# A decoder layer's expert inputs: each weight tile against 256-column activations in three products, gelu straight from PSUM

## The chip, the cores and the metric

The kernel runs on one core of one Trainium2 chip. What counts is the device time of one execution in microseconds (us). Five engines work side by side: TensorE (PE, with its weight loads listed apart as PEld), VectorE (DVE), ScalarE (ACT), GpSimd (POOL) and SyncE (SP), which issues most DMA transfers.

## What is computed

One layer of a decoder with 256 tokens and 2048 channels. It has an attention and a convolution branch, and then a layer of experts. The change touches the expert layer only. Cut to that, the reference is:

```
h2 = rms_norm(x, norm2_g) * (1 + scale2) + shift2
q = h2 @ w_q;  s = q . sub_keys           # scores, 8 heads x 2 halves x 128 keys
gate, expert = top 16 of 16 x 16 pairs, softmax over the scores
a = einsum('td,ted->te', h2, u_emb[expert])
coef = gelu(a) * gate
out = x + gate2 * einsum('te,ted->td', coef, v_emb[expert])
```

There are 128 x 128 = 16384 experts, and `u_emb` and `v_emb` have a row of 2048 for each.

## The kernel before

The experts are not gathered. The kernel computes the gelu of every expert's input for every token, multiplies it by a gate that is zero where the expert was not chosen, and multiplies the result by all of `v_emb`. So the expert layer is dense: 128 tiles of 128 experts against h2 (the **expert-input stage**, `u_tile`, called 128 times), and then all coefficients against `v_emb` (the **output stage**, `products`).

All large weights come through one class, `Stream`. SP loads chunks of 128 x 1024 floats (`raw`, four buffers). For each 512 columns of a chunk ACT casts the numbers to a shorter float (`hi`, L153, five buffers) and DVE subtracts to get the rest (`lo`, L159, four buffers), so that a product of two floats is made of three products of short ones: hi x hi, hi x lo and lo x hi. `prefetch` issues these casts three pieces ahead. A **piece** is the use of one such 512-column pair: four blocks of the contraction with 128 weight columns each. A weight tile of 128 experts is four pieces (16 blocks of 128 channels).

`proj` (L200 to L202) is the usual form: for each block one 256-column product of `hi` with the high activations, one of `hi` with the low ones, one of `lo` with the high ones. Each has its own weight load. The query heads (`head_q`), among others, use it. `proj2` (L213, L217) is used by `u_tile` alone. There h2 lies in one tile with the high and the low activations of a block side by side, so `hi` meets both in one 512-column product, and the sums are in the two halves of a PSUM bank; `lo` then meets the high ones in 256 columns.

After each piece, `step` moves the jobs on that stand in a list; a job is a generator that issues a few instructions and yields. So the order of instructions on all engines is fixed by the program, by how many pieces have gone by. The jobs in the expert-input stage are

- the evacuation of each tile (`f` in `u_tile`): ACT (the first 48 tiles) or DVE copies the second half of the bank into `ut`, DVE adds the first half, and ACT takes the gelu into the coefficient tile `C`. Where gates are already there (`n` tokens of 256), it is taken in two parts, and DVE multiplies the first part into `C`;
- in the first 48 tiles, `top_steps` on DVE: the top 16 of each head;
- then `g_steps`, 64 times: for four tokens, DVE makes one-hot tiles, ACT scales them, PE multiplies them (L1247, eight products of 128 columns in f16, the **one-hot products**) and DVE and ACT bring the result into `C`.

The scores of a head are one small group of f32 products (L1078, eight passes, the **head product**); that of the last head is issued within the first tile of the expert-input stage. Three pairs of transposes (L1140) come at the end of `top_steps`.

Of the kernel before, what the change touches and what calls it, by code (L numbers as in the profile page):

```python
# [9 lines left out]
F32 = mybir.dt.float32  # L10
F32R = mybir.dt.float32r
F16 = mybir.dt.float16
U32 = mybir.dt.uint32
AF = mybir.ActivationFunctionType
# [5 lines left out]
T = 256  # L20
D = 2048
KT = 16
# [50 lines left out]
def build(nc, tc, d):  # L73
    ctx = ExitStack()
    ve, sc, pe, sp = nc.vector, nc.scalar, nc.tensor, nc.sync
# [53 lines left out]
    class Stream:  # L129
# [63 lines left out]
        def proj(self, bank, nk, xhi, xlo, evac):  # L193

            ps = bank()
            for k0 in range(0, nk, 4):
                def mm(hi, lo):
                    for j in range(4):
                        k, o = k0 + j, j * 128
                        pe.matmul(ps, hi[:, o:o + 128], xhi[:, k], start=(k == 0), stop=False)  # L200
                        pe.matmul(ps, hi[:, o:o + 128], xlo[:, k], start=False, stop=False)  # L201
                        pe.matmul(ps, lo[:, o:o + 128], xhi[:, k], start=False, stop=(k == nk - 1))  # L202
                self.piece(mm)
            return self.add(evac(ps))

        def proj2(self, bank, nk, x, evac):

            ps = bank()
            for k0 in range(0, nk, 4):
                def mm(hi, lo):  # L210
                    for j in range(4):
                        k, o = k0 + j, j * 128
                        pe.matmul(ps.rearrange("p a t -> p (a t)"), hi[:, o:o + 128],  # L213
                                  x[:, k].rearrange("p a t -> p (a t)"), start=(k == 0), stop=False)
                    for j in range(4):
                        k, o = k0 + j, j * 128
                        pe.matmul(ps[:, 1], lo[:, o:o + 128], x[:, k, 0], start=False, stop=(k == nk - 1))  # L217
                self.piece(mm)
            return self.add(evac(ps))

# [33 lines left out]
    S = Stream(plan)  # L254
# [37 lines left out]
    def bank_st(shape):  # L292
        return ps_st.tile(shape, F32, name="ps_st", tag="st", bufs=1)

    ps = bank_st([128, T])
# [175 lines left out]
    def gen_bank(shape, tag="t", bufs=2):  # L471
        return ps_mix.tile(shape, F32, name="ps_" + tag, tag=tag, bufs=bufs)
# [470 lines left out]
    UC = T + 2  # L943
    gg = P("gg", side="right")
    h2p = P("h2p", side="right")
    h2 = h2p.tile([128, KT, 2, T], F32R, name="h2")
    h2hi, h2lo = h2[:, :, 0], h2[:, :, 1]
    np_ = P("np", side="right")
    rs2 = np_.tile([128, T], F32, name="rs2")
    hgate = np_.tile([128, 16], F32, name="hgate")  # L950
# [92 lines left out]
    HALF = 48  # L1043
# [143 lines left out]
    tokens, ready = [0], [0]  # L1187

    def u_tile(i1):
        def f(ps):  # L1190
            n = tokens[0]
            cs = C[0][:, i1] if i1 < HALF else C[1][:, i1 - HALF]
            t = gg.tile([128, T], F32, name="ut", tag="ut", bufs=1)
            if i1 < HALF:
                sc.copy(t, ps[:, 1])
            else:
                ve.tensor_copy(t, ps[:, 1])
            yield
            ve.tensor_add(t, t, ps[:, 0])
            yield  # L1200
            n = tokens[0]
            if n < T:
                sc.activation(cs[:, n:], t[:, n:], AF.Gelu_apprx_tanh)
            if n > 0:
                sc.activation(t[:, 0:n], t[:, 0:n], AF.Gelu_apprx_tanh)
            ready[0] = i1 + 1
            yield
            if n > 0:
                ve.tensor_mul(cs[:, 0:n], cs[:, 0:n], t[:, 0:n])
            yield  # L1210
        return S.proj2(lambda: gen_bank([128, 2, T], "acc"), KT, h2, f)

    def g_steps():

# [57 lines left out]
    for i1 in range(HALF):  # L1272
        u_tile(i1)
# [16 lines left out]
    for i1 in range(HALF, NK):  # L1290
        end = u_tile(i1)
# [164 lines left out]
```

## Time and profile before

| | us |
|---|---|
| median of 3 runs | 2449.55 |
| lowest, highest | 2449.41, 2452.64 |
| the profiled execution | 2450.68 |
| its span, first to last instruction | 2448.9 |
| PE busy | 2424.4 (99%) |
| DVE busy | 1935.9 (79%) |
| ACT busy | 1433.1 (59%) |

The profile shows one execution. The length of a matmul in it is longer than its share of the time, since matmuls overlap: a 256-column one is shown with some 0.28 us and the next one starts 0.11 us after it. What a stretch of matmuls costs is therefore read from the starts in the timeline, or from a window's length and the count of matmuls in it.

### The profile page before, as it was taken

What the parts mean: (1) busy time and instruction counts of PE and PEld (TensorE: products, weight loads), DVE (VectorE), ACT (ScalarE), POOL (GpSimd) and SP (SyncE); (2) the same over time, 40 slices, a digit from 0 to 9 for tenths busy, and PEclk for the clock granted to TensorE, in tenths of its full rate; (3) what the DMA queues carried; (4) which work ended last, traced back from release to release, by engine and by line L of the source; (5) the groups of instructions that cost most, each with busy time, mean ns of one, the idle gap of its engine ahead of it and who ended that gap; (6) DMA issues with size and microseconds to landing.
All of it is one profiled execution on the core that took longest, in us unless ns stands there. A gap on an engine that the chain in (4) does not pass through costs nothing.

```text
span 2448.9 us, 44266 instructions
## 1 busy us (share of the span) xinstructions
PE 2424.4 (99%) x15324; PEld 2151.9 (88%) x15324; DVE 1935.9 (79%) x4120; ACT 1433.1 (59%) x3214; POOL 144.0 (6%) x269
## 2 busy tenths in 40 slices
PE   8999999999999999999999999999999999999999
PEld 6899999888999999988888888888888888888887
DVE  7979887889788877999988888888655566666666
ACT  2145456767555566555568888888555555555554
POOL 0000000211222200000000000000000001000100
PEclk9999999999999999999999999999999999999999
DMA  9966556755899975555555555555555567777766
GB/s 384 405 217 197 178 190 196 241 176 186 301 319 322 319 263 173 184 190 190 191 184 177 176 177 176 174 178 174 191 191 193 190 211 244 240 245 240 243 205 195
DMA packets 155668, 540.50 MB, mean 221 GB/s; under 512 B 18866, under 2 KB 19122, under 8 KB 155314
## 3 DMA queue, kind: packets, MB, share of 16 engines
q1 hardware_dynamic: 134178, 467.40, 56.2%
q0 software_dynamic: 21264, 70.27, 9.3%
q8 instruction: 120, 1.97, 0.3%
q14 instruction: 106, 0.86, 0.1%
HBM read 533.41 MB, written 4.19 MB: 220 GB/s over the span
## 4 chain that ended last, share of the span: by engine, by line
PE 92%; DMA 4%; DVE 3%; issue 1%; SPq 0%; ACT 0%; DVEq 0%
PE ps_acc L213 20%; PE ps_acc L217 10%; PE acc L200 9%; PE acc L202 9%; PE acc L201 9%; DMA wa<-in_w_ada_dram 4%; PE ps_o L1335 2%; PE ps_s L1335 2%; PE ps_t L1335 2%; PE ps_o L1334 2%; PE ps_s L1334 2%; PE ps_t L1334 2%; PE ps_acc L1335 2%; PE ps_acc L1334 2%; PE ps_t L1336 2%; PE ps_o L1336 2%
## 5 line engine op out<-in xcount | busy, mean ns | idle before, releaser
L153 ACT CAST hi<-raw 128x512 fp32r<-128x512 f32 x1548 | 954.2, 620 | 802.2 <-PE acc L201 228.7
L159 DVE TENSOR_TENSOR lo<-raw,hi 128x512 fp32r<-128x512 f32 x1548 | 1064.4, 689 | 387.3 <-ACT hi L153 80.2
L213 PE MATMUL ps_acc<-h,hi 128*128 128x512 f32 x2048 | 564.6, 397 | 0.0
L213 PEld LDWEIGHTS ps_acc<-h,hi 128*128 128x128 f32 x2048 | 347.0, 188 | 44.2
L217 PEld LDWEIGHTS ps_acc<-h,lo 128*128 128x128 f32 x2048 | 311.5, 188 | 46.1
L200 PE MATMUL acc<-hhi,hi 128*128 128x256 f32 x1200 | 345.9, 288 | 0.0
L202 PE MATMUL acc<-hhi,lo 128*128 128x256 f32 x1200 | 333.0, 278 | 0.2 <-DVE lo L159 0.2
L201 PE MATMUL acc<-hlo,hi 128*128 128x256 f32 x1200 | 333.0, 277 | 0.0
L217 PE MATMUL ps_acc<-h,lo 128*128 128x256 f32 x2048 | 318.1, 277 | 0.0
L200 PEld LDWEIGHTS acc<-hhi,hi 128*128 128x128 f32 x1200 | 225.9, 188 | 6.3 <-issue 5.3
L201 PEld LDWEIGHTS acc<-hlo,hi 128*128 128x128 f32 x1200 | 226.1, 188 | 3.2 <-issue 3.1
L202 PEld LDWEIGHTS acc<-hhi,lo 128*128 128x128 f32 x1200 | 225.4, 188 | 0.4 <-DVE lo L159 0.4
L391 POOL DMA_DIRECT2D adaw<-in_w_ada_dram x192 | 104.7, 546 | 760.5 <-DVE rr L739 276.9
L405 DVE SCALAR_TENSOR_TENSOR ada<-adaw,sc_c,ada 128x512 f32<-128x512 f32 x180 | 134.5, 747 | 13.6 <-DMA adaw<-in_w_ada_dram 13.3
L1311 POOL DMA_DIRECT2D g2w<-in_w_ada_dram x64 | 34.3, 537 | 1404.4 <-DVE Alo L123 1098.5
L491 DVE SCALAR_TENSOR_TENSOR cacc<-glu,dwh,cacc 128x256 f32<-128x256 f32 x240 | 107.2, 491 | 0.0
L1226 ACT ACTIVATE Ahi<-ohA,high 128x128 f16<-128x128 f16 x256 | 100.7, 393 | 10.9 <-PE ps_o L1247 10.5
L359 PE MATMUL zb<-hr,w 128*128 128x256 f32 x448 | 103.9, 391 | 3.1 <-ACT hr L339 3.1
L359 PEld LDWEIGHTS zb<-hr,w 128*128 128x128 f32 x448 | 86.1, 195 | 15.0 <-ACT hr L339 3.4
L1226 ACT ACTIVATE Alo<-ohA,low 128x128 f16<-128x128 f16 x256 | 99.1, 387 | 0.0
L323 DVE SCALAR_TENSOR_TENSOR acc<-wa,sc_c,acc 128x256 f32<-128x256 f32 x224 | 91.3, 480 | 2.1 <-DMA wa<-in_w_ada_dram 2.1
L200 PE MATMUL acc<-mhi,hi 128*128 128x256 f32 x256 | 71.5, 279 | 0.0
(371 smaller groups left out, 4529.9 us busy)
## 6 DMA issues: line engine op xcount, KB each, us to landing
raw<-in_u_dram SPq DMA_DIRECT2D x256, 512.0 KB, 3.6
raw<-in_v_dram SPq DMA_DIRECT2D x256, 512.0 KB, 4.6
raw<-in_w_in_dram SPq DMA_DIRECT2D x150, 512.0 KB, 4.3
adaw<-in_w_ada_dram POOLq DMA_DIRECT2D x192, 256.0 KB, 5.1
wa<-in_w_ada_dram SPq DMA_DIRECT2D x64, 512.0 KB, 9.9
raw<-in_nsa_out_dram SPq DMA_DIRECT2D x32, 512.0 KB, 6.2
raw<-in_w_out_dram SPq DMA_DIRECT2D x32, 512.0 KB, 5.4
raw<-in_peer_wq_dram SPq DMA_DIRECT2D x32, 512.0 KB, 4.1
```

What stands on the lines that cost most here:

```text
L153: sc.copy(hi, self.source(n))
L159: ve.tensor_sub(lo, self.source(n), hi.bitcast(F32))
L200: pe.matmul(ps, hi[:, o:o + 128], xhi[:, k], start=(k == 0), stop=False)
L201: pe.matmul(ps, hi[:, o:o + 128], xlo[:, k], start=False, stop=False)
L202: pe.matmul(ps, lo[:, o:o + 128], xhi[:, k], start=False, stop=(k == nk - 1))
L213: pe.matmul(ps.rearrange("p a t -> p (a t)"), hi[:, o:o + 128], x[:, k].rearrange("p a t -> p (a t)"), start=(k == 0), stop=False)
L217: pe.matmul(ps[:, 1], lo[:, o:o + 128], x[:, k, 0], start=False, stop=(k == nk - 1))
L359: pe.matmul(zb[n // 2][:, n % 2], ws[k][n // 7][:, n % 7], hr[k], start=(k == 0 and n % 2 == 0), stop=(k == KT - 1), skip_group_check=True)
L405: ve.scalar_tensor_tensor(acc, raw, sc_c[:, k:k + 1], acc, op0=OP.mult, op1=OP.add)
L1226: sc.activation(part[:, j], A[:, j], AF.Copy, scale=g[:, t0 + j:t0 + j + 1])
L1334: pe.matmul(ps, chi, hi, start=(i1 == 0), stop=False)
L1335: pe.matmul(ps, chi, lo, start=False, stop=False)
```

## The change

`proj2` goes, and `u_tile` calls `proj` on two separate tiles, `h2hi` and `h2lo`. A tile's PSUM is 256 columns wide, and gelu reads it directly; the copy and the addition go.

```diff
-        def proj2(self, bank, nk, x, evac):
-
-            ps = bank()
-            for k0 in range(0, nk, 4):
-                def mm(hi, lo):
-                    for j in range(4):
-                        k, o = k0 + j, j * 128
-                        pe.matmul(ps.rearrange("p a t -> p (a t)"), hi[:, o:o + 128],
-                                  x[:, k].rearrange("p a t -> p (a t)"), start=(k == 0), stop=False)
-                    for j in range(4):
-                        k, o = k0 + j, j * 128
-                        pe.matmul(ps[:, 1], lo[:, o:o + 128], x[:, k, 0], start=False, stop=(k == nk - 1))
                 self.piece(mm)
             return self.add(evac(ps))
...
-    h2 = h2p.tile([128, KT, 2, T], F32R, name="h2")
-    h2hi, h2lo = h2[:, :, 0], h2[:, :, 1]
+    h2hi = h2p.tile([128, KT, T], F32R, name="h2hi")
+    h2lo = h2p.tile([128, KT, T], F32R, name="h2lo")
...
             cs = C[0][:, i1] if i1 < HALF else C[1][:, i1 - HALF]
-            t = gg.tile([128, T], F32, name="ut", tag="ut", bufs=1)
-            if i1 < HALF:
-                sc.copy(t, ps[:, 1])
-            else:
-                ve.tensor_copy(t, ps[:, 1])
-            yield
-            ve.tensor_add(t, t, ps[:, 0])
-            yield
-            n = tokens[0]
             if n < T:
-                sc.activation(cs[:, n:], t[:, n:], AF.Gelu_apprx_tanh)
+                sc.activation(cs[:, n:], ps[:, n:], AF.Gelu_apprx_tanh)
             if n > 0:
-                sc.activation(t[:, 0:n], t[:, 0:n], AF.Gelu_apprx_tanh)
+                t = gg.tile([128, T], F32, name="ut", tag="ut", bufs=1)
+                sc.activation(t[:, 0:n], ps[:, 0:n], AF.Gelu_apprx_tanh)
             ready[0] = i1 + 1
...
-        return S.proj2(lambda: gen_bank([128, 2, T], "acc"), KT, h2, f)
+        return S.proj(lambda: gen_bank([128, T], "acc"), KT, h2hi, h2lo, f)
```

How the order of instructions changes is seen best on PE. First at the beginning of the expert-input stage, from its first product to the head product (L1078 before, L1063 after) and a little beyond; `acc` and `ps_acc` are the PSUM tiles, `h_10305` is the interleaved h2. Before:

```order
L202 MATMUL acc<-h_10305,lo 128x256
L213 MATMUL ps_acc<-h_10305,hi 128x512 x4
L217 MATMUL ps_acc<-h_10305,lo 128x256 x4
L213 MATMUL ps_acc<-h_10305,hi 128x512 x4
L217 MATMUL ps_acc<-h_10305,lo 128x256 x4
L1078 MATMUL ps_s<-skT,pq 128x128 x4
L213 MATMUL ps_acc<-h_10305,hi 128x512 x4
L217 MATMUL ps_acc<-h_10305,lo 128x256 x4
```

And now, from the last two blocks ahead of the head product on:

```order
L200 MATMUL ps_acc<-h2hi,hi 128x256
L201 MATMUL ps_acc<-h2lo,hi 128x256
L202 MATMUL ps_acc<-h2hi,lo 128x256
L200 MATMUL ps_acc<-h2hi,hi 128x256
L201 MATMUL ps_acc<-h2lo,hi 128x256
L202 MATMUL ps_acc<-h2hi,lo 128x256
L1063 MATMUL ps_s<-skT,pq 128x128 x4
L200 MATMUL ps_acc<-h2hi,hi 128x256
L201 MATMUL ps_acc<-h2lo,hi 128x256
L202 MATMUL ps_acc<-h2hi,lo 128x256
```

The head product stays where it was, after two pieces; each piece has twelve products of one width in place of four wide and four narrow ones.

Second on PE, in the later part of the stage, the end of the one-hot products (L1247 before, L1224 after) and what follows them. Before:

```order
L1247 LDWEIGHTS ohB
L1247 MATMUL ps_o<-Ahi,ohB 128x128
L1247 LDWEIGHTS ohB
L1247 MATMUL ps_o<-Alo,ohB 128x128
L213 MATMUL ps_acc<-h_10305,hi 128x512 x4
L217 MATMUL ps_acc<-h_10305,lo 128x256 x4
```

And now:

```order
L1224 LDWEIGHTS ohB
L1224 MATMUL ps_o<-Ahi,ohB 128x128
L1224 LDWEIGHTS ohB
L1224 MATMUL ps_o<-Alo,ohB 128x128
L200 MATMUL ps_acc<-h2hi,hi 128x256
L201 MATMUL ps_acc<-h2lo,hi 128x256
L202 MATMUL ps_acc<-h2hi,lo 128x256
```

What follows an interruption is now a run of 256-column products.

On DVE, a tile in the later part of the stage (`C_13041` and `C_16353` are the two halves of the coefficients). Before:

```order
L1197 COPY ut<-ps_acc 128x256
L159 TENSOR_TENSOR lo<-raw,hi 128x512
L1220 TENSOR_TENSOR ohB<-cst,I2T 128x512
L1199 TENSOR_TENSOR ut<-ut,ps_acc 128x256
L159 TENSOR_TENSOR lo<-raw,hi 128x512
L1235 TENSOR_TENSOR C_13041<-C_13041,ps_o 128x48x4
L1235 TENSOR_TENSOR C_16353<-C_16353,ps_o 128x51x4
L159 TENSOR_TENSOR lo<-raw,hi 128x512
L1209 TENSOR_TENSOR C_16353<-C_16353,ut 128x176
```

And now:

```order
L159 TENSOR_TENSOR lo<-raw,hi 128x512
L1197 TENSOR_TENSOR ohB<-cst,I2T 128x512
L1186 TENSOR_TENSOR C_16981<-C_16981,ut 128x172
L159 TENSOR_TENSOR lo<-raw,hi 128x512
L1212 TENSOR_TENSOR C_13042<-C_13042,ps_o 128x48x4
L1212 TENSOR_TENSOR C_16981<-C_16981,ps_o 128x52x4
```

The copy and the addition are gone, and the product with the gates stands two pieces earlier. SP's transfers keep their order.

## Rows read from the trace of the kernel before

**Rows 1.** The page: busy us, share of the span, instructions; granted clock in tenths.

```profile
PE 2424.4 (99%) x15324; PEld 2151.9 (88%) x15324; DVE 1935.9 (79%) x4120; ACT 1433.1 (59%) x3214; POOL 144.0 (6%) x269
...
PEclk9999999999999999999999999999999999999999
```

**Rows 2.** Windows: stretch, length, busy us (count) of PE, PEld, DVE, ACT, POOL; clock.

```profile
1002.00:1252.00 250.00, 250.00 (x1443) 218.33 (x1442) 236.45 (x711) 142.12 (x272) 0.00 (x0) 1.00 0.58 190
1272.00:1740.00 468.00, 468.00 (x3013) 410.19 (x3013) 384.85 (x801) 374.88 (x1035) 0.00 (x0) 1.00 0.54 177
1741.00:2009.00 268.00, 268.00 (x1173) 219.94 (x1172) 152.82 (x248) 136.51 (x245) 2.12 (x4) 1.00 0.60 195
2010.00:2400.00 390.00, 390.00 (x1722) 322.88 (x1722) 266.47 (x426) 201.11 (x361) 32.19 (x60) 1.00 0.72 235
```

**Rows 3.** The tile `ut`: count; ns least/median/most; first and last start; forms.

```profile
L1199 DVE TENSOR_TENSOR ut<-ut,ps_acc x128: 399/414/419, 1004.4 to 1742.4; 128x256 f32<-128x256 f32 x128
L1203 ACT ACTIVATE C<-ut x123: 193/370/421, 1006.0 to 1715.2; 128x256 f32<-128x256 f32 x49, 128x240 f32<-128x240 f32 x2, 128x216 f32<-128x216 f32 x2, 128x192 f32<-128x192 f32 x2
L1197 DVE COPY ut<-ps_acc x80: 415/419/425, 1269.4 to 1741.2; 128x256 f32<-128x256 f32 x80
...
L1195 ACT COPY ut<-ps_acc x48: 354/367/368, 1001.8 to 1263.3; 128x256 f32<-128x256 f32 x48
```

**Rows 4.** Timeline of PE, steady pieces: start us, length us, engine, line, count.

```profile
1102.81 1.09 PE L213 MATMUL ps_acc<-h,hi 128*128 128x512 f32 x4
1103.74 0.62 PE L217 MATMUL ps_acc<-h,lo 128*128 128x256 f32 x4
...
1111.13 1.09 PE L213 MATMUL ps_acc<-h,hi 128*128 128x512 f32 x4
```

**Rows 5.** Timeline of PE behind the last head product.

```profile
997.90 1.05 PE L1078 MATMUL ps_s<-skT,pq 128*128 128x128 f32 x8
...
999.72 0.63 PE L217 MATMUL ps_acc<-h,lo 128*128 128x256 f32 x4
1000.19 1.10 PE L213 MATMUL ps_acc<-h,hi 128*128 128x512 f32 x4
```

**Rows 6.** Timeline of PE at one set of one-hot products.

```profile
1406.11 0.23 PE L1247 MATMUL ps_o<-Ahi,ohB 128*128 128x128 f16 x1
...
1406.54 1.18 PE L213 MATMUL ps_acc<-h,hi 128*128 128x512 f32 x4
1407.56 0.62 PE L217 MATMUL ps_acc<-h,lo 128*128 128x256 f32 x4
1408.02 1.09 PE L213 MATMUL ps_acc<-h,hi 128*128 128x512 f32 x4
```

**Rows 7.** Timeline of PE, query heads: first and last of three stretches.

```profile
963.65 0.28 PE L200 MATMUL acc<-h,hi 128*128 128x256 f32 x1
...
973.74 0.28 PE L202 MATMUL acc<-h,lo 128*128 128x256 f32 x1
...
975.10 0.28 PE L200 MATMUL acc<-h,hi 128*128 128x256 f32 x1
...
985.81 0.28 PE L201 MATMUL acc<-h,hi 128*128 128x256 f32 x1
...
987.64 0.28 PE L200 MATMUL acc<-h,hi 128*128 128x256 f32 x1
...
995.01 0.28 PE L202 MATMUL acc<-h,lo 128*128 128x256 f32 x1
```

**Rows 8.** Timeline of PE behind four transposes: first and last of a stretch.

```profile
633.00 0.28 PE L201 MATMUL acc<-hlo,hi 128*128 128x256 f32 x1
...
665.87 0.28 PE L200 MATMUL acc<-ohi,hi 128*128 128x256 f32 x1
```

**Rows 9.** Timeline: one `lo`, and the first products of its piece.

```profile
1199.84 0.68 DVE L159 TENSOR_TENSOR lo<-raw,hi 128x512 fp32r<-128x512 f32 x1
...
1202.65 1.09 PE L213 MATMUL ps_acc<-h,hi 128*128 128x512 f32 x4
```

More of the change, by code (lines that the diff above doesn't have):

```diff
@@ L202, in mm @@
                         pe.matmul(ps, lo[:, o:o + 128], xhi[:, k], start=False, stop=(k == nk - 1))
-                self.piece(mm)
-            return self.add(evac(ps))
-        def proj2(self, bank, nk, x, evac):
-            ps = bank()
-            for k0 in range(0, nk, 4):
-                def mm(hi, lo):
-                    for j in range(4):
-                        k, o = k0 + j, j * 128
-                        pe.matmul(ps.rearrange("p a t -> p (a t)"), hi[:, o:o + 128],
-                                  x[:, k].rearrange("p a t -> p (a t)"), start=(k == 0), stop=False)
-                    for j in range(4):
-                        k, o = k0 + j, j * 128
-                        pe.matmul(ps[:, 1], lo[:, o:o + 128], x[:, k, 0], start=False, stop=(k == nk - 1))
                 self.piece(mm)
```

## The prediction

> **What bounds the kernel now.** I read the page first: PE is busy for 99% of the span and the granted clock is full in every slice [rows 1]. Since busy time of pipelined matmuls says little, I went on to the stage that the change touches. The expert-input stage runs from about 995 to 1740 us. In the windows inside it PE shows no idle time, while DVE and ACT both have some [rows 2]; the waits of PE in this stretch are an empty list. So the stage lasts as long as its matmuls take from start to start, and I need their pace, which the timeline gives.
>
> I call the work on one quarter of a weight tile (four k blocks, one `hi` and one `lo` tile) a piece. 128 expert tiles of 4 pieces make 512 pieces. A piece before is four 512-column products (L213) and four 256-column products (L217). Six pieces in a row begin at 1102.81 and end at 1111.13, so a piece lasts 1.387 us: 0.93 for the four wide products, 0.457 for the four narrow ones [rows 4]. The window agrees: 250 us hold 1443 matmuls, 8 a piece, 1.386 us each [rows 2]. In the second part, from about 1271 us, the one-hot products (eight f16 matmuls, 64 times) cut in: 0.43 us, and the wide group behind them takes 1.02 instead of 0.93, so 0.52 us a time [rows 6]. Check: 3013 matmuls, 8 a piece and 8 an interruption, are 376.6 of both, and at 1.387 and 0.52 us the 468 us contain 63 interruptions [rows 2].
>
> **What the new piece costs.** It is twelve 256-column products, each with its own weight load, the form that `proj` already runs in the query heads just ahead, on the same h2. There the trace shows two paces (columns of the rows: start, length, engine, line). From 963.65 to 973.74 there are 90 such matmuls, 89 gaps of 113.4 ns; from 975.10 to 985.81 there are 92, 91 gaps of 117.7 ns [rows 7]. Both have a granted clock of 2.4 GHz, the same form and the same tiles. I call them the short and the long pace. Twelve of the short make 1.360 us a piece, twelve of the long 1.413 us: 0.027 us less or 0.026 us more than before. Over 512 pieces that is -13.8 or +13.3 us, so the whole question is which pace the stage falls into.
>
> What chooses? In these rows the pace changes only where other matmuls cut in (the head's eight short f32 passes, L1078) and then holds. Between these two stretches stands one head product; behind the next one it is short again, 66 matmuls with 65 gaps of 113.4 ns from 987.64 to 995.01 [rows 7]: the sides alternate. Behind transposes in an earlier stage the short pace held for 291 matmuls, 290 gaps of 113.3 ns, from 633.00 to 665.87 [rows 8].
>
> First part of the stage, up to the first one-hot product at about 1271 us. The last head product is issued two pieces into the stage, in the old order and the new one, and the stretch ahead of it is short; by alternation it is followed by the long pace. The old rows agree: behind that product (997.90) the four narrow matmuls take 0.47 us, which is 4 x 117.7, against 0.45 to 0.46 in the steady state [rows 4, 5]. Before, the wide products then bring the pattern back; in the new stream nothing follows but more 256-column products, until three pairs of transposes shortly before 1271 us. So I take the long pace for 190 pieces: 190 x 0.026 = +4.9 us. If it broke at once it would be 190 x -0.027 = -5.1 us.
>
> Second part, 320 pieces. Behind the one-hot products the wide group is 0.09 us late and the narrow group takes 0.46 us, not 0.47 [rows 6]: the pattern comes back on the short side. I read that as the short pace for the new stream: 320 x -0.027 = -8.6 us. No 256-column product of this type stands behind f16 ones in the trace, so both ends stay open: +8.3 us if it is long each time. I keep the 0.09 us for the restart and add 0.01 us (two gaps at the long pace) 64 times, +0.6 us; the ends are nothing and +2.3 us (eight long gaps).
>
> **Edits at nothing.** 48 ACT copies of 0.367 us, 80 DVE copies of 0.419 and 128 DVE additions of 0.414 go [rows 3]: 17.6, 33.5 and 53.0 us of engine time, all beside a PE that does not pause [rows 2], so 0. The cover is PE itself: were the feeders late, this would be the reserve. The two gelus read PSUM where they read `ut`; a copy from PSUM on ACT costs 0.367 us, a gelu from SBUF 0.370 [rows 3], so a moved read costs nothing either. The gelu now waits on ACT for the last matmul of its tile. Queued behind it are the casts to `hi`. But the cast just ahead of it waits for the same piece to give its buffer back, so nothing is added.
>
> What gets tighter is the weights. `lo` was first read 0.93 us into a piece and is now read by the third matmul, 0.23 us in; `hi` is given back by the eleventh of twelve matmuls, at 1.25 us, not at 0.93. In the piece with the least lead, in the first part where DVE is busy 236 of 250 us, `lo` ends at 1200.52 and the piece begins at 1202.65 [rows 2, 9]. That leaves 2.13 + 0.23 = 2.36 us where the new stream needs it, and DVE has 53 us less to do, so I charge 0. If it failed, the price would be a stop of some tenths of a us in up to 190 pieces. Weights are cast and loaded no faster and SP's queue gets the same transfers in the same order.
>
> The four query heads on h2 read two tiles in place of one interleaved tile, rows of 1 KB in both. 32 pieces, two heads at each pace: 0, with +-0.9 us if a head changes sides. In the output stage the first stretch runs at 268 us for 1173 matmuls and the next at 390 for 1722 [rows 2], 228.5 and 226.5 ns each; the change of pace falls where the coefficients move to another pool. In the changed kernel the first pool's tiles lie 1 KB lower. I take 0; at the faster pace it would be 1173 x -2 ns = -2.3 us, and at twice 117.7 ns it would be +8 us.
>
> **Sum.** +4.9 - 8.6 + 0.6 = -3.1 us, taken from the profiled execution's 2450.68 us: 2447.6. That execution lies 1.1 us over the median of the runs, 2449.55, so I predict 2446.5 us.
>
> **Rivals.**
> All short: the new stream settles in the short pace behind the head product too, or falls back to it soon. For: both paces hold with the same tiles, and transposes led to the short one [rows 8]. Against: the alternation and the 0.47 us. 510 x -0.027 + 0.6 = -13.2, so 2436.4 us. Where the long pace breaks midway it is between this and the forecast.
>
> All long: the f16 products leave the stream on the long side each time, as the f32 head products did [rows 5, 7]. Place: 320 pieces behind 64 interruptions; price 0.026 us each, on top of the first part: 510 x 0.026 = +13.3, so about 2462.8 us. It is slower than before from the point where more than half of all pieces are long. The Trainium skill (TensorE: Matmul & The Clock Gate, section Back-to-back issue gap) speaks for this side: it gives each matmul a fixed cost of some 2.5 ns on top of its columns, which favours few wide products. By its cycle table a piece before would be 1.300 us and one after 1.310, an estimate of +5 us. The trace does not show a fixed cost: 226.5 ns for 512 columns [rows 2] are exactly two times 113.3.
>
> Half and half: the one-hot products make the sides alternate, as the head products do. First part +4.9, second 160 x 0.026 - 160 x 0.027 = -0.2, with the restarts about +5: 2454.8 us.
>
> **How the numbers follow.** I give my forecast 0.46, all short (with the broken middle) 0.25, half and half 0.13, all long 0.16. A run of this kernel can be told from no change at about 0.2%, here 4.9 us, so 2444.7 to 2454.4. Of the forecast, 0.03 goes to faster through the output stage's term and a break of the long pace; the rest is the same. All short is faster; half and half sits on the bound and is split; all long is slower. That gives faster 0.28, same 0.49, slower 0.23. The forecast's own range is 2444 to 2450 us. The range for 8 in 10 reaches from 2434 (all short with the output stage's gain) to 2458, which holds half and half and a second part that is mostly long at its lower edge, and leaves out most of all long.
>
> **What would show it.** In the timeline of the changed kernel: the gap between 256-column products behind the last head product (117.7 expected) and behind the one-hot products (113.3); the window of the first part should hold 12 matmuls in 1.413 us, later 1.360. PE should have no wait for `lo`. A PE that pauses for `lo` or `hi`, a third pace, or a changed pace in the output stage would make the prediction wrong, as would the long pace behind the one-hot products.

## The result: 0.8% slower, outside the range

The changed kernel takes 2471.69 us (median of 4 runs, 2468.38 to 2472.38), the kernel before 2451.1 beside it: a ratio of 1.0077, with a 95% interval of 1.0065 to 1.0088. I had forecast 2446.5 us with a range up to 2458. The profiled execution took 2468.38 us, its span is 2466.6, 17.7 more than before.

I read the same four stretches as [rows 2]; all but the first begin some us later now, so their windows are shifted. The columns are those of [rows 2].

```profile
1002.00:1252.00 250.00, 250.00 (x2126) 250.00 (x2124) 222.50 (x657) 124.02 (x223) 0.00 (x0) 1.00 0.56 186
1272.00:1750.00 478.00, 478.00 (x4292) 475.16 (x4291) 340.94 (x647) 372.81 (x1042) 0.00 (x0) 1.00 0.53 174
1760.00:2028.00 268.00, 268.00 (x1150) 217.11 (x1149) 149.45 (x240) 133.83 (x240) 2.12 (x4) 1.00 0.58 192
2030.00:2410.00 380.00, 380.00 (x1679) 314.74 (x1678) 259.39 (x414) 195.35 (x349) 32.21 (x60) 1.00 0.71 235
```

PE is busy throughout at full clock, as before, and the list of its waits from 1000 to 1750 us is empty. In the first window 250 us hold 2126 matmuls, twelve a piece: 1.411 us a piece, the long pace. In the third, 268 us hold 1150 products of 512 columns: 233.0 ns each, against 228.5 in [rows 2]. In the last it is 226.3, against 226.5. So every stretch but the last became slower, on a PE that never stopped.

The timeline of PE shows where the pace is set. Behind the head product (columns as in [rows 4]), two products in the steady stream, and around the first set of one-hot products and the next:

```profile
997.53 1.05 PE L1063 MATMUL ps_s<-skT,pq 128*128 128x128 f32 x8
998.34 0.36 PE L200 MATMUL ps_acc<-h2hi,hi 128*128 128x256 f32 x1
...
1102.07 0.28 PE L201 MATMUL ps_acc<-h2lo,hi 128*128 128x256 f32 x1
...
1109.84 0.28 PE L201 MATMUL ps_acc<-h2lo,hi 128*128 128x256 f32 x1
...
1276.50 0.22 PE L1224 MATMUL ps_o<-Alo,ohB 128*128 128x128 f16 x1
1276.53 0.36 PE L200 MATMUL ps_acc<-h2hi,hi 128*128 128x256 f32 x1
1276.73 0.28 PE L201 MATMUL ps_acc<-h2lo,hi 128*128 128x256 f32 x1
1276.85 0.28 PE L202 MATMUL ps_acc<-h2hi,lo 128*128 128x256 f32 x1
1276.97 0.28 PE L200 MATMUL ps_acc<-h2hi,hi 128*128 128x256 f32 x1
...
1283.56 0.28 PE L202 MATMUL ps_acc<-h2hi,lo 128*128 128x256 f32 x1
1283.68 0.23 PE L1224 MATMUL ps_o<-Ahi,ohB 128*128 128x128 f16 x1
```

From 1102.07 to 1109.84 there are 66 gaps of 117.7 ns. Behind the one-hot products the first gap is 0.20 us, and then the gaps are 0.12 again; from 1276.73 to 1283.56 there are 58 of 117.8. Each of the 64 sets is followed by the long pace, without exception. That is the point at which I had taken the short one.

For all kernels below I give three lengths from the starts in the timeline: the expert-input stage from its first product to the first one-hot product (**A**), from there to the first output product (**B**), and the output stage from there until the coefficients move to the other pool (**C**). The rest of the output stage is 433.2 to 433.3 us in all of them.

| kernel | time, us | A | B | C |
|---|---|---|---|---|
| before (profiled) | 2450.68 | 276.18 | 469.12 | 269.17 |
| changed (profiled) | 2468.38 | 281.29 | 476.85 | 274.40 |
| one_tile | 2466.58 | 281.29 | 476.85 | 274.40 |
| ut_first | 2472.66 | 281.29 | 476.85 | 274.40 |
| before_ut_last | 2449.66 | 276.18 | 469.12 | 269.19 |
| kick_survey | 2479.99 | 291.28 | 476.85 | 274.40 |
| old_evac | 2462.56 | 281.29 | 476.85 | 269.19 |
| kick_two | 2461.67 | 281.40 | 476.88 | 269.27 |
| kick_onehot | 2472.06 | 281.29 | 480.42 | 269.19 |
| wide_then_narrow | 2451.07 | 276.18 | 469.17 | 269.24 |
| late_wide | 2447.56 | 271.34 | 469.12 | 269.19 |
| mixed | 2454.85 | 271.27 | 475.78 | 269.19 |
| wide_kicks | 2471.53 | 271.91 | 492.23 | 269.19 |
| columns | 2469.09 | 282.22 | 475.77 | 274.40 |
| short16 | 2444.75 | 272.02 | 467.57 | 269.17 |

Changed minus before is +5.1, +7.7 and +5.2: 18.1 us from the unrounded starts. The spans of the two profiled executions differ by 17.7, since the stage begins 0.3 us earlier in the changed kernel. The medians differ by 20.6, with an interval of some 16 to 22, in which the lengths' sum lies. Times of late_wide, mixed and short16 are medians of 11 or 12 runs, of the other experiments one run, which moves by some us; the lengths repeat to about 0.1 us, so I judge by those. Letters in the expectations below name theories: C, L and S there are not the length C or the paces L and S.

### The profile page after: what moved, and what is told of

It reads as the page before. It is cut to its first block, busy times and chain, and to the rows that moved or that the text cites. A ratio compares the mean times of both kernels' runs of the same rounds, so it can differ in the third digit from the quotient of the medians.

```text
span 2466.6 us, 48249 instructions
## 1 busy us (share of the span) xinstructions
PE 2442.7 (99%) x17372; PEld 2256.5 (91%) x17372; DVE 1879.3 (76%) x3912; ACT 1413.7 (57%) x3166; POOL 144.1 (6%) x269
## 4 chain that ended last, share of the span: by engine, by line
PE 92%; DVE 4%; DMA 3%; issue 0%; ACT 0%; SPq 0%; DVEq 0%
PE ps_acc L200 10%; PE ps_acc L202 10%; PE ps_acc L201 10%; PE acc L200 9%; PE acc L202 9%; PE acc L201 9%; DMA wa<-in_w_ada_dram 3%; PE ps_o L1313 2%; PE ps_s L1313 2%; PE ps_t L1313 2%; PE ps_o L1311 2%; PE ps_o L1312 2%; PE ps_s L1312 2%; PE ps_t L1312 2%; PE ps_s L1311 2%; PE ps_t L1311 2%
## 5 line engine op out<-in xcount | busy, mean ns | idle before, releaser
L200 PE MATMUL ps_acc<-h2hi,hi 128*128 128x256 f32 x2048 | 581.1, 284 | 0.0
L202 PE MATMUL ps_acc<-h2hi,lo 128*128 128x256 f32 x2048 | 575.3, 281 | 0.0
L201 PE MATMUL ps_acc<-h2lo,hi 128*128 128x256 f32 x2048 | 575.3, 281 | 0.0
L201 PEld LDWEIGHTS ps_acc<-h2lo,hi 128*128 128x128 f32 x2048 | 390.7, 191 | 0.0
L200 PEld LDWEIGHTS ps_acc<-h2hi,hi 128*128 128x128 f32 x2048 | 387.1, 189 | 0.0
L202 PEld LDWEIGHTS ps_acc<-h2hi,lo 128*128 128x128 f32 x2048 | 384.4, 188 | 0.0
L201 PE MATMUL acc<-hlo,hi 128*128 128x256 f32 x1200 | 332.8, 277 | 0.0
L201 PEld LDWEIGHTS acc<-hlo,hi 128*128 128x128 f32 x1200 | 226.1, 188 | 3.2 <-issue 3.1
```

## The experiments

### Is it where the tiles lie, or what the stream went through?

The change also moves tiles in memory. Theory P says that their place sets the pace, theory H that the stream's own history does. Four kernels:

```diff
 one_tile: the changed kernel, with
-    h2hi = h2p.tile([128, KT, T], F32R, name="h2hi")
-    h2lo = h2p.tile([128, KT, T], F32R, name="h2lo")
+    h2 = h2p.tile([128, KT, 2, T], F32R, name="h2")
+    h2hi, h2lo = h2[:, :, 0], h2[:, :, 1]
 ut_first: the changed kernel, in u_tile's f, ahead of gelu
+            if i1 == 0:
+                gg.tile([128, T], F32, name="ut", tag="ut", bufs=1)
 before_ut_last: the kernel before, ahead of the first tile
+    for nm in ("I1T", "I2T"):
+        gg.tile([128, T], F16, name=nm)
+    ...
 kick_survey: the changed kernel, behind tiles 2 to 45
+        if 2 <= i1 < 46:
+            kick(KICKS[i1 % len(KICKS)])
```

A kick is one to four unread instructions on PE: transpositions (t1 to t4), f32 products (m1, m2, m4), products of 512 (w1, w2) or of 128 columns (n1, n2) of the short float.

> The changed kernel with h2 in one interleaved tile as before, and nothing else undone: the same three products, gelu from PSUM. H expects no difference: pace 117.8 ns all through the expert-input stage, stage 758 us against 745 before, output stage as in the changed kernel. P, in the form that the separate tiles slow the products down, expects the short pace, a stage of about 732 us.

> The changed kernel with the tile ut allocated first in its pool, so that ohA, ohB, Ahi and Alo lie where they lay before (1 KB higher). The first part of the output stage took 269.2 us before (228.9 ns a product) and 274.4 us in the changed kernel (233.3 ns). P expects 228.9 ns and 269.2 us again, total 5 us under the changed kernel. H (the long pace is handed on by the stage ahead) expects 233.3 ns and 274.4 us. Both expect the expert-input stage unchanged at 758 us.

> The kernel before with the tile ut allocated last in its pool, so that ohA, ohB, Ahi and Alo lie where the changed kernel has them (1 KB lower), and nothing else changed. P expects the first part of the output stage at 233.3 ns a product, 274.4 us, total 5 us over the kernel before. H expects 228.9 ns and 269.2 us, total unchanged at 2450 us. Both expect the expert-input stage unchanged at 745 us.

> The changed kernel with a few extra products on PE behind each of the tiles 2 to 45 of the expert-input stage (one to four transposes, one, two or four f32 products of 128 columns, one or two short-float products of 512 columns or of 128); nothing reads their sums. Theory H (history): the pace of the 256-column products, 113.3 or 117.8 ns from start to start, is a state of the stream that an interruption can switch and that holds until the next one, with the same tiles. It expects stretches at both paces behind the kicks, switching only at them, and the stretches at the long side again behind the same kind of kick when they were short before, or the other way round. Theory P (place): the pace follows from where the operands lie, and the new tiles h2hi and h2lo have the long one. It expects 117.8 ns behind every kick, as in the changed kernel, and a first part of 281.3 us plus the kicks' own time (some 44 x 0.3 = 13 us).

The first three keep A, B and C of their base to 0.02 us: P falls for these moves. In kick_survey the pace changed behind kicks and nowhere between them, both ways, with the same tiles in the same place (L is the long pace and S the short one, ahead of the kick and behind it, four of each):

```
t1 L>S 4        t2 S>L 4        t3 L>S 3, L>L 1   t4 S>L 3, L>S 1
m1 L>L 3, S>S 1 m2 L>L 3, S>S 1 m4 L>S 3, S>S 1
w1 S>S 4        w2 S>S 4        n1 S>L 4          n2 L>L 4
```

So within the expert-input stage the pace is latched, as H says: in no run does a stretch of 256-column products change it before something cuts in. The output stage is another matter. Where the coefficients move to the other pool, at the end of C, the gaps of the changed kernel go from 233 to 227 ns within nine products, and nothing else stands between these products on PE. No run tells what does this; tiles in another place are one candidate. The first set of one-hot products was met on the short side here, and was followed by the long pace all the same; B is as long as in the changed kernel. I read off that the kind of the interruption chooses, and the next runs were to use that.

### The evacuation, and two kicks put to use

```diff
 old_evac: the changed kernel, in u_tile's f
+            t = gg.tile([128, T], F32, name="ut", tag="ut", bufs=1)
+            if i1 < HALF:
+                sc.copy(t, ps)
+            else:
+                ve.tensor_copy(t, ps)
+            yield
+            ve.tensor_tensor(t, t, ps, op=OP.max)
+            yield
+    ... gelu then reads t
 kick_two: a transposition behind tile 1, one ahead of the output stage
 kick_onehot: a transposition behind each set
                         pe.matmul(ps[:, j], B[:, j], parts[i][:, j], ...)
+                kick()
 wide_then_narrow: the kernel before, ahead of the output stage
+    pe.matmul(ps[:, 0:128], h2[:, 0, 0, 0:128], h2[:, 0, 0, 0:128], ...)
```

> The changed kernel with the old evacuation put back: each expert-input result is copied out of PSUM, then a VectorE operation reads the copy and the bank once more (a maximum of equal values, in the old addition's place), and gelu reads the copy. Theory H (the pace of the products is set by what interrupted their stream last): no engine but TensorE is the bound, so the expert-input stage stays at 281.3 + 476.9 us and the output stage's first part at 274.4; time 2471 within 3. Theory E (gelu's direct read of PSUM holds banks or slows the stream): the stage would come back towards 276.2 + 469.1 us and the time to about 2455.

> The changed kernel with two added 128x128 transpositions of the identity, whose result nobody reads: one behind the expert-input stage's second tile, one between the last expert-input product and the first output product. Theory H: the first flips the stream behind the head product to the short pace, so the part up to the first one-hot product goes from 281.3 to 272 us (182 pieces by 0.053 less); the one-hot products put it back, so the rest stays at 476.9; the second flips the output stage's first part from 274.4 to 269.2 us or below (228.9 ns a 512-column product instead of 233.3); time about 2453 to 2457. Rival C (the lengths belong to the code or data of each stage, not to what came before): all three stay within 0.5 us of the changed kernel's, time 2471.

> The changed kernel with one added 128x128 transposition of the identity, unread, behind the one-hot products of each of the 64 token sets. Theory H: each puts the stream back to the short pace, so the 320 pieces behind them lose 0.053 us each (17 us) and 64 transpositions cost 0.1 to 0.25 each (6 to 16): the rest of the expert-input stage goes from 476.9 to 466 to 476 us; a 256-column product starts 113.3 ns behind the one before instead of 117.7; the output stage, entered from the short pace, takes 269.2 or less instead of 274.4; time 2457 to 2467. Rival C: the pace stays at 117.7 ns behind every set, and the 64 transpositions add 6 to 16 us, time 2477 to 2487.

> The kernel before, unchanged but for one added 128-column product of high activations by themselves, unread, between the last expert-input product and the first output product. Theory H: such a product flipped a short stream to the long pace in 4 of 4 cases, so the output stage's first part takes 274.4 us instead of 269.2 and all else stays (276.2 and 469.1); time about 2455. Rival C: the output stage stays at 269.2 us, time 2450. Rival S (only the wide products ahead of it decide, a single narrow one is forgotten): also 269.2.

Three windows of the changed kernel, and the same of old_evac:

```profile
1020.00:1250.00 230.00, 230.00 (x1956) 230.00 (x1955) 205.04 (x606) 112.47 (x203) 0.00 (x0) 1.00 0.56 186
1300.00:1700.00 400.00, 400.00 (x3601) 397.52 (x3600) 289.11 (x554) 318.28 (x898) 0.00 (x0) 1.00 0.52 174
1770.00:2000.00 230.00, 230.00 (x987) 186.33 (x986) 127.87 (x206) 114.86 (x206) 0.00 (x0) 1.00 0.57 188
```

```profile
1020.00:1250.00 230.00, 230.00 (x1956) 230.00 (x1955) 214.96 (x648) 126.47 (x244) 0.00 (x0) 1.00 0.56 186
1300.00:1700.00 400.00, 400.00 (x3601) 397.52 (x3601) 327.66 (x685) 323.01 (x900) 0.00 (x0) 1.00 0.52 174
1770.00:2000.00 230.00, 230.00 (x1006) 188.75 (x1005) 130.18 (x210) 116.94 (x210) 0.00 (x0) 1.00 0.57 191
```

The old evacuation adds 10 and 39 us of DVE work in the first two windows, and PE does the same number of matmuls, 1956 and 3601. So the edit is worth nothing in the expert-input stage, as I had it, and theory E falls. But in the output stage old_evac does 1006 products instead of 987: C is short. The first output products show where they part; the changed kernel, then old_evac:

```profile
1752.95 0.40 PE L1311 MATMUL ps_o<-hi,ohA 128*128 128x512 f32 x1
1753.18 0.40 PE L1312 MATMUL ps_o<-lo,ohA 128*128 128x512 f32 x1
1753.42 0.40 PE L1313 MATMUL ps_o<-hi,ohB 128*128 128x512 f32 x1
1753.65 0.40 PE L1311 MATMUL ps_o<-hi,ohA 128*128 128x512 f32 x1
```

```profile
1752.35 0.40 PE L1319 MATMUL ps_o<-hi,ohA 128*128 128x512 f32 x1
1752.59 0.39 PE L1320 MATMUL ps_o<-lo,ohA 128*128 128x512 f32 x1
1752.82 0.39 PE L1321 MATMUL ps_o<-hi,ohB 128*128 128x512 f32 x1
1753.05 0.40 PE L1319 MATMUL ps_o<-hi,ohA 128*128 128x512 f32 x1
1753.28 0.39 PE L1320 MATMUL ps_o<-lo,ohA 128*128 128x512 f32 x1
1753.52 0.39 PE L1321 MATMUL ps_o<-hi,ohB 128*128 128x512 f32 x1
```

Both come from the long pace and nothing cuts in. In the changed kernel the gaps are 236, 233, 233, 234 ns and stay so. C holds 49 x 24 = 1176 products: 274.40 us are 233.3 ns each and 269.17, before, 228.9, and the 4.4 between them are the same 4.4 as between 117.7 and 113.3. In old_evac they are 235, 231, 229, 237, 232, 231, and from then on 226, 229 and 232 in turn, as before. So here the long pace was left within six products though nothing cut in. What does it I can't say: kick_onehot and mixed show it too, and kick_onehot hasn't the old evacuation.

The transpositions did not do what they did in the survey. Behind tile 1 (kick_two) the pace stayed long; behind the sets (kick_onehot) it was short for the first two, and long for the other 62. In wide_then_narrow a product that had gone S>L four times changed nothing. C of kick_two is short as H expected, but with old_evac beside it that shows little. So the latch of the expert-input stage stands, and my reading that the kind of an interruption chooses its outcome falls.

### The old form for a part of the tiles

The next guess, theory L: a wide product leaves the short pace. Against it N: a stream of 256-column products alone comes back to the long one.

```diff
 late_wide: the kernel before, u_tile's end
+        if 0 < i1 < HALF:
+            return S.proj(lambda: gen_bank([128, T], "acc"), KT, h2hi, h2lo, narrow)    # narrow: ... gelu from PSUM
         return S.proj2(lambda: gen_bank([128, 2, T], "acc"), KT, h2, f)
 mixed: the same, and in tiles 48 to 127 a piece has
+                    n = 4 if wide[0] else 1 if k0 == 0 else 0    # wide: behind a set
+                    for j in range(4):
+                        if j < n: ... one 512-column product
+                        else: ... two of 256 columns
 wide_kicks: the changed kernel, a 512-column product behind tile 1,
             behind each set and ahead of the output stage
```

> The kernel before, with expert-input tiles 1 to 47 (those ahead of the one-hot products) by three 256-column products and gelu read from PSUM, and tile 0 and tiles 48 to 127 by the old wide products and evacuation; h2 stays one tile. Theory L (the pace is latched by what the last interruption left, and a wide product leaves the short pace): tile 0's wide products, behind the head product, lead to the short pace, so tiles 1 to 47 take 1.360 us a piece instead of 1.387: the part up to the first one-hot product 271.5 to 272 us instead of 276.2, the rest 469.1 and the output stage's first part 269.2 as before; time 2445 to 2447, faster than both. Rival N (256-column products alone always come to the long pace in this stage): that part takes 280 to 281 us, time 2454.

> As late_wide up to tile 47; in tiles 48 to 127 the piece behind each set of one-hot products is wide, as is the first high product of each tile (it starts both halves of the bank), and all other products there are of 256 columns; old evacuation in these tiles. Theory L: the wide piece behind the one-hot products leaves the short pace for the 256-column pieces up to the next set, so some 256 of 320 pieces take 0.027 us less than before: the rest of the stage 461 to 465 us instead of 469.1, the part ahead of it 271.5 to 272, the output stage 269.2; time 2437 to 2442. Rival N: the 256-column pieces there stay on the long pace, the rest of the stage takes 474 to 477 us and the part ahead 280; time 2459 to 2463.

> The changed kernel with an added product of 512 columns (two k blocks of the high activations, unread) behind tile 1, behind the one-hot products of each of the 64 sets, and ahead of the output stage. Theory L: each leads to the short pace: the part up to the first one-hot product 271.5 to 272.5 us instead of 281.3; the 256-column products behind the sets start 113.3 ns apart instead of 117.7, and that part takes 476.9 - 17.0 + 64 x 0.235 = 474.9 us (460 without the 64 products' own time); the output stage's first part 269.2 or less instead of 274.4; time about 2455. Rival N: the pace stays long, 281.5 + 492 us, output stage 274.4, time about 2487.

Late_wide does what L expects. A window of it in A, and below it one of mixed in B:

```profile
1020.00:1250.00 230.00, 230.00 (x2032) 230.00 (x2031) 210.72 (x620) 118.63 (x212) 0.00 (x0) 1.00 0.61 195
```

```profile
1300.00:1700.00 400.00, 400.00 (x3336) 385.69 (x3335) 328.45 (x686) 322.55 (x899) 0.00 (x0) 1.00 0.52 174
```

Late_wide holds 2032 matmuls in the first 230 us, 113.2 ns each, where the changed kernel holds 1956; A is 4.8 us shorter than before. It is faster than before: 0.9981 (0.9972 to 0.9990). Mixed has the same A, but its B is as N expects: the ratio to before is 1.0009 (1.0000 to 1.0018). Its timeline of PE at the first wide products of tiles 48 and 49 (L216):

```profile
1263.33 0.28 PE L202 MATMUL ps_acc<-h,lo 128*128 128x256 f32 x1
1263.45 0.39 PE L216 MATMUL ps_acc<-h,hi 128*128 128x512 f32 x1
1263.68 0.28 PE L219 MATMUL ps_acc<-h,hi 128*128 128x256 f32 x1
...
1268.44 0.62 PE L223 MATMUL ps_acc<-h,lo 128*128 128x256 f32 x4
1268.90 0.39 PE L216 MATMUL ps_acc<-h,hi 128*128 128x512 f32 x1
1269.12 0.28 PE L219 MATMUL ps_acc<-h,hi 128*128 128x256 f32 x1
1269.24 0.28 PE L220 MATMUL ps_acc<-h,hi 128*128 128x256 f32 x1
1269.36 0.28 PE L219 MATMUL ps_acc<-h,hi 128*128 128x256 f32 x1
```

The first of them took the stream from the long pace to the short one: the 46 products from 1263.68 to the next L216 at 1268.90 take 113.4 ns each. The second, the same product one tile on, took it back: 119, 117, 117, 118 ns behind it. The wide pieces behind the sets, issued just as in [rows 6], leave 118, 117, 118 and 0.47 us for four narrow products, not the 0.45 to 0.46 of the kernel before; the first of them:

```profile
1272.15 1.17 PE L216 MATMUL ps_acc<-h,hi 128*128 128x512 f32 x4
1273.16 0.63 PE L223 MATMUL ps_acc<-h,lo 128*128 128x256 f32 x4
1273.63 0.28 PE L219 MATMUL ps_acc<-h,hi 128*128 128x256 f32 x1
```

In wide_kicks the product behind tile 1 gave the short pace and the 64 behind the sets never did. So L holds in A, and falls in B.

### One size after the other

My next guess was that neither kind nor neighbour decides, but the few ns that an interruption leaves between the products around it. That is theory T; a sweep over one size tests it. K: behind one-hot products the pace is long whatever follows. R: chance.

```diff
 columns: the changed kernel, behind tiles 2 to 41 and behind each set in turn
+    COLS = (16, 32, 64, 96, 128, 160, 192, 224, 288, 320, 352, 384, 416, 448, 480, 512, -1, -2, -3, -4)
+        if n > 0:
+            pe.matmul(ps[:, 0:n], h2hi[:, 0, 0:128], h2hi[:, 0:2].rearrange("p a t -> p (a t)")[:, 0:n], ...)
+        for j in range(-n):
+            pe.transpose(ps[:, j * 128:(j + 1) * 128], ident, ident)
```

> The changed kernel with one unread product of n columns (16, 32, 64, ... 512: sixteen sizes), or one to four unread transpositions, in turn behind each of tiles 2 to 41 and behind the one-hot products of each of the 64 sets. Theory T (the pace is latched; an interruption switches it or not by how many ns it leaves between the two products around it and by the pace on which it is met, whatever its kind): behind the tiles the result goes both ways, by size, and one size met on one pace gives the same result both times; behind the one-hot products at least some sizes give the short pace, repeatedly. Rival K (behind one-hot products nothing but a stream of wide products gives the short pace): all 64 stretches behind the sets stay at 117.7 ns a product. Rival R (chance): the same size on the same pace gives different results. Time 2471 plus some 10 us of added products, less 0.23 us for every stretch of 5 pieces on the short pace.

Behind the sets each of the twenty had one outcome in all of its three or four rounds: the long pace for 96, 320, 416, 448 and 512 columns, the short one for the other eleven sizes and for the transpositions (48 short stretches, 16 long). Behind the tiles 18 of 20 gave the same outcome both times; t3, met on the long pace both times, gave S and then L, and t4 differed with it. Two restarts, with 16 and with 96 columns:

```profile
1421.25 0.26 PE L1242 MATMUL ps_t<-h2hi 128*128 128x16 f32 x1
1421.36 0.36 PE L200 MATMUL ps_acc<-h2hi,hi 128*128 128x256 f32 x1
1421.56 0.28 PE L201 MATMUL ps_acc<-h2lo,hi 128*128 128x256 f32 x1
1421.67 0.28 PE L202 MATMUL ps_acc<-h2hi,lo 128*128 128x256 f32 x1
...
1422.58 0.28 PE L201 MATMUL ps_acc<-h2lo,hi 128*128 128x256 f32 x1
...
1443.56 0.29 PE L1242 MATMUL ps_t<-h2hi 128*128 128x96 f32 x1
1443.69 0.35 PE L200 MATMUL ps_acc<-h2hi,hi 128*128 128x256 f32 x1
1443.88 0.28 PE L201 MATMUL ps_acc<-h2lo,hi 128*128 128x256 f32 x1
1443.99 0.28 PE L202 MATMUL ps_acc<-h2hi,lo 128*128 128x256 f32 x1
...
1444.94 0.28 PE L201 MATMUL ps_acc<-h2lo,hi 128*128 128x256 f32 x1
```

From the first L201 to the next one shown are nine gaps: 1.02 us and 1.06, 113 and 118 ns, 80 columns apart. K falls. Chance doesn't explain outcomes that repeat for all twenty behind the sets, though behind the tiles t3 did what R expects. T holds only in part: size matters, and repeatably, though each size was met on the pace that the one before it had left. A transposition behind a set, met on the long pace, gave S three of three times here and L 61 of 62 times in kick_onehot. In both kernels 615 ns lie between the 256-column products around it (from 1393.16 to 1393.78 us in columns, from 1382.28 to 1382.90 in kick_onehot, to name one of each). So neither the visible pace nor the whole ns in between, T's two terms, fix the outcome.

### The short pace throughout

With 16 columns behind a set the first gaps are 200, 114, 113 at once. This run was to tell whether the pace is the whole of the loss:

```diff
 short16: the changed kernel, with a product of 16 columns behind tile 2 and behind each set
+        pe.matmul(ps[:, 0:16], h2hi[:, 0, 0:128], h2hi[:, 0, 0:16], start=True, stop=True)
```

> The changed kernel with one unread product of 16 columns behind tile 2 and behind the one-hot products of each of the 64 sets (in the columns run that size gave the short pace behind the sets in 4 of 4 cases, and behind the tiles from the long pace in 2 of 2). Theory T: the part up to the first one-hot product 271.5 to 272.5 us instead of 281.3; a set and its added product take 0.107 us more than the set alone (659 ns to 552 between the 256-column products around them), so the rest of the stage takes 476.9 - 17.0 + 6.9 = 466.7 us; the output stage's first part, entered from the short pace, 269.2; time 2443 to 2446, faster than the kernel before by 0.2 to 0.3%. Rival Q (a size gives the same pace only behind the sizes that stood before it in that run; by itself it falls back to the long pace, as the transposition did): the rest of the stage 476.9 + 6.9 = 483.7 us, time 2462 to 2468. Rival O (the pace isn't the whole loss): the paces are short and the sum still stays above 2448.

```profile
1020.00:1250.00 230.00, 230.00 (x2032) 230.00 (x2032) 211.78 (x626) 117.38 (x212) 0.00 (x0) 1.00 0.59 194
1300.00:1700.00 400.00, 400.00 (x3726) 397.97 (x3725) 293.86 (x562) 321.38 (x911) 0.00 (x0) 1.00 0.53 177
1770.00:2000.00 230.00, 230.00 (x1007) 188.71 (x1006) 130.17 (x210) 117.17 (x210) 2.12 (x4) 1.00 0.59 194
```

All 64 stretches behind the sets are short; 400 us hold 3726 matmuls instead of 3601, the added ones among them. The time is 2444.75 us, 0.9974 of before (0.9965 to 0.9983), so it beats that too; with 65 more products than the changed kernel, its A, B and C are 23.8 us shorter in sum. A and C are where T has them, and B is 0.9 us over. So the pace is enough to explain the whole of the loss, and O and Q fall. Whether short16 or late_wide is better is not told apart: their intervals overlap.

## Why the prediction was wrong

**The step that failed** is the second part. I wrote of the old rows behind the one-hot products that "the pattern comes back on the short side", and "I read that as the short pace for the new stream": -8.6 us, with +0.6 for restarts. Measured is +7.7, next to the other end that I had named, +8.3. That is 15.7 us of the 21 by which the lengths missed the sum. The reading was sound for the old stream, but I carried it over to a stream in which the wide products are gone. Mixed shows how little it bears: the same old wide piece behind the same one-hot products left the long pace. The latch I had from [rows 7, 8], but no row of before has 256-column products of this type behind f16 ones, so none could tell the outcome. "Both ends stay open" was the right sentence, and the weight on one of them the mistake.

**The output stage.** I took 0 with -2.3 and +8 as ends. Measured is +5.2: 4.4 ns on each product. It is the second term that was mis-sized. I did name twice 117.7 ns as the upper end, but tied the term to where the tiles lie. The 1 KB did nothing (ut_first, before_ut_last). In the changed kernel the stage is on the long pace from its first products, as the stage ahead was; but old_evac, kick_onehot and mixed came from the long pace too and left it. Why the changed kernel keeps it stays open.

**First part: right.** The long pace behind the head product, +4.9 forecast and +5.1 measured. My reason, that the sides alternate, is weaker than its outcome: behind the sets they don't alternate, and in kick_survey they do only for some kinds. There m4, eight f32 passes as in the head product, left a short stream short. So this term came out right partly by luck.

**Edits at nothing: right in their stage.** Copies and additions were hidden (old_evac), gelu from PSUM holds nothing up, and PE has no wait for `lo`. The read from PSUM is not dearer either. Of the part that goes through `ut`, the five of 256 columns took 414 ns on average before and take 380 now; all of them, before and now (columns as in [rows 3]):

```profile
L1205 ACT ACTIVATE ut<-ut x79: 193/303/415, 1278.1 to 1743.9; 128x256 f32<-128x256 f32 x5, 128x16 f32<-128x16 f32 x2, 128x40 f32<-128x40 f32 x2, 128x64 f32<-128x64 f32 x2
L1182 ACT ACTIVATE ut<-ps_acc x79: 158/272/393, 1282.1 to 1753.6; 128x256 f32<-128x256 f32 x5, 128x8 f32<-128x8 f32 x2, 128x28 f32<-128x28 f32 x2, 128x52 f32<-128x52 f32 x2
```

**The rivals.** All long is what came: 2462.8 us, and with the output stage's 5.2 it is 2468.0, against a median of 2471.69 and 2468.38 for the profiled execution. It had a chance of 0.16, and my range ended at 2458. All short exists: late_wide's A is 271.34, 4.8 under before, where 190 x 0.027 gave 5.1. The Trainium skill (TensorE: Matmul & The Clock Gate, section Back-to-back issue gap), whose formula for a matmul by itself speaks for few wide products, has the sign of the result but not its cause: on the short pace the twelve 256-column products are faster than the wide form, in A of late_wide and of short16.

## What to carry over

Where a stream of equal matmuls shows two paces at the same clock, a change that takes other shapes out of it is worth either of them: price both, give neither much more than half, and let the range hold both. Compare stage lengths from the starts, not times; they repeat to 0.1 us where single runs move by some us, and they show which stage has which pace. When a stream is on the long side, one tiny product at a place that cuts it anyway is worth a try, a few sizes in one run; it must be looked at in the trace again after any other edit.

## What was not expected of the hardware

- The two paces lie 4.4 ns a product apart at 256 columns (113.3 and 117.7) and at 512 (228.9 and 233.3), at a granted clock of 1.00 in all these windows. At 512 columns there is a third one: 226.3 to 226.5 in the rest of the output stage, before and now.
- Behind the same eight f16 products, one more product of 64, 96 or 128 columns gave short, long and short, in every round (met on the short, the short and the long pace).
- An added product of 16 or of 32 columns costs the same: between the 256-column products around a set lie 659 ns with either, 552 without.
- What decides the pace behind an interruption, and what ends it in the output stage without one, stays open.
